# The second feed-forward product by Strassen's algorithm, in four quarters

## The chip, the core and the metric

The kernel runs on one core of one Trainium2 chip. The core has five engines that work side by side, each with a queue of its own that it takes in order: TensorE (PE) for matrix products, VectorE (DVE), ScalarE (ACT) and GpSimd (POOL) for passes over tiles, and SyncE (SP), which issues transfers. PE reads its operands from SBUF, the on-chip memory of 128 partitions, and writes to PSUM, eight banks of 128 x 512 floats; ACT and DVE bring results from there. The metric is the device time of one execution in microseconds (us). Times of single instructions come from one profiled execution.

## The reference

One layer of a streaming encoder runs over 512 tokens of width 1024. Three branches (banded attention, a gated recurrence, latent attention) are gated, summed and added to the residual. Then comes the feed-forward part, in which the change lies, and a last norm:

```python
h2 = rmsnorm(x, norm_ffn_g)
x = x + jnp.square(jax.nn.relu(h2 @ w_ff1)) @ w_ff2     # w_ff1: 1024 x 4096, w_ff2: 4096 x 1024
return rmsnorm(x, final_norm_g)
```

## The kernel before

All products have float32 accuracy made of three matmuls: each operand is split into a high part of the short float format fp32r and a low part (the rest), and high times high, high times low and low times high are added in PSUM (`mm3`, lines 223 to 226). `gemm` (line 228) does that over the 128-row blocks of the inner dimension. Activations lie transposed, features on partitions and the 512 tokens along the free dimension, so a weight block of 128 x 128 is PE's stationary operand and 512 tokens stream past it.

`stream` (line 213) brings a weight tile of 128 x 1024: SP loads it into `wr` (two buffers), ACT casts it into `wh`, DVE subtracts into `wl` (three buffers each). In the first part of the kernel, the projections, weights come in another way (`convert`, line 271): POOL issues a load of the weight, ACT negates its high part, and a second POOL transfer adds the weight to it in flight.

The feed-forward part begins at line 1154. The loop of line 1163 makes the residual `x2` (eight tiles of 128 features by 512 tokens) with `w_out`, and its scaled high and low parts `x2g`. The norm's factor per token goes through the squared ReLU, so it is applied only at the end, as `rs2`, its square. Then two halves of 2048 hidden features (line 1186): 16 products of `w_ff1` (24 matmuls of 512 columns each), relu on ACT, square on DVE and a split into `rh` and `rl`; then, for each of eight output tiles, products with `w_ff2`. The first half's 16 blocks and the third group of eight are kept as sums in `y0`. The last group's weights are split ahead (`wres`, line 1213), and its products run over 256 tokens at a time (line 1245), so that the first 256 tokens can be finished while the others are still on PE. To finish (line 1253 on) is: multiply by `rs2`, add to the residual, square for the last norm's sum, scale by the final gain on POOL; `finish_half` (line 1230) sums the squares over partitions by fp32 matmuls with a matrix of ones, makes the reciprocal root on ACT and DVE, multiplies the eight tiles (six on DVE, two on POOL) and stores them in four transfers.

PE's order is that of the code. The other queues are ordered when the program is built, by a planner that runs through the program with estimated durations and takes, for each engine, the first in priority among the instructions that are ready. Priority is the order of the code; what stands under `urgent()` (the weights) counts as 6000 places earlier.

Of the kernel before, what the change touches and what calls it, by code (L numbers as in the profile page):

```python
# [9 lines left out]
F32 = mybir.dt.float32  # L10
# [6 lines left out]
D = 1024  # L17
S = 512
# [24 lines left out]
def _blocks(w, nk, cols):  # L43

    c = w.shape[1] // cols
    return w.reshape(nk, P, c, cols).transpose(2, 1, 0, 3).reshape(c, P, nk * cols)
# [30 lines left out]
def layout(inp):  # L77
# [34 lines left out]
    o['w_out'] = _blocks(f('w_out')[0], NK, P)  # L112
    o['w_ff1'] = _blocks(f('w_ff1')[0], NK, P)
    w2 = f('w_ff2')[0]
    o['w_ff2'] = np.stack([_blocks(w2[c * 1024:(c + 1) * 1024], NK, P) for c in range(4)])
    freq = (np.float32(10000.0) ** (-np.arange(0, 32, 2, dtype=np.float32) / np.float32(32))).astype(np.float32)
    sg = np.where(np.arange(P) % 32 < 16, -1.0, 1.0).astype(np.float32)
    o['cst'] = np.concatenate([
# [20 lines left out]
def _body(ctx, tc, ap, dbgo):  # L139
# [22 lines left out]
    def acc(n="acc"):  # L162
        return ps.tile([P, S], F32, tag="acc", name=n, bufs=3)
# [990 lines left out]
    with ExitStack() as f_ctx:  # L1154
        fp = f_ctx.enter_context(tc.tile_pool(name="ffn", bufs=2, reuse_waits="tile"))

        def fw(n):
            return fp.tile([P, S], F32, tag="fw", name=n, bufs=3)


        x2, x2g = [], []
        ss = fp.tile([P, S], F32, name="fss", bufs=1)
        for m in range(NK):
            x = fqt("xres")
            nc.sync.dma_start(x, ap['xT'][m * P:(m + 1) * P, :])
            w = stream(ap['w_out'][m], eng=V)
            pz = acc("po")
            gemm(pz, w, mT, NK)
            V.tensor_tensor(x, pz, x, ALU.add)
            dbg('x2', x, m)  # L1170
            xh = fp.tile([P, S], F32R, tag="xg", name="x2h", bufs=16)
            xl = fp.tile([P, S], F32R, tag="xg", name="x2l", bufs=16)
            A.activation(xh, x, AF.Copy, scale=g_ffn[:, m:m + 1])
            V.scalar_tensor_tensor(xl, x, g_ffn[:, m:m + 1], f(xh), ALU.mult, ALU.subtract)
            x2g.append((xh, xl))
            sq = ss if m == 0 else fw("sq")
            A.activation(sq, x, AF.Square)
            if m:
                G.tensor_tensor(ss, ss, sq, ALU.add)
            x2.append(x)  # L1180
        t6 = tables("natural_log_exp_and_others", last_copy)
        rs2 = fp.tile([P, S], F32, name="rs2", bufs=1)


        y0 = []
        for half in range(2):
            rT = []
            for j in range(16):
                w = stream(ap['w_ff1'][half * 16 + j], eng=V)
                pz = acc("p1")  # L1190
                gemm(pz, w, x2g, NK)
                t = fw("t")
                A.activation(t, pz, AF.Relu)
                V.tensor_tensor(t, t, t, ALU.mult)
                rh = fp.tile([P, S], F32R, tag="r", name="rh", bufs=32)
                rl = fp.tile([P, S], F32R, tag="r", name="rl", bufs=32)
                split(rh, rl, t)
                rT.append((rh, rl))
                if half == 0 and j == 1:
                    pst = psc("pst")  # L1200
                    T.matmul(pst, ones, ss, start=True, stop=True)
                    A.activation(rs2, rstd_of(fw, pst, D, behind=t6), AF.Square)
            for m in range(NK):
                pz = acc("p2")
                gemm(pz, stream(ap['w_ff2'][2 * half, m], eng=V), rT, NK, stop=half == 1)
                if half == 0:
                    gemm(pz, stream(ap['w_ff2'][1, m], eng=V), rT[8:], NK, start=False)
                    t = act.tile([P, S], F32, tag="act", name="y0")
                    A.copy(t, pz)
                    y0.append(t)  # L1210
                else:
                    V.tensor_tensor(y0[m], y0[m], pz, ALU.add)
        wres = []
        for m in range(NK):
            if m >= 6:
                hi, lo = stream(ap['w_ff2'][3, m], eng=V)
                wres.append([(hi[:, i * S:(i + 1) * S], lo[:, i * S:(i + 1) * S]) for i in range(2)])
                continue
            r = ws.tile([P, 1024], F32, tag="wr", name="wr", bufs=2)
            nc.sync.dma_start(r, ap['w_ff2'][3, m])  # L1220
            hl = []
            for i in range(2):
                if m < 2:
                    hi, lo = (act.tile([P, S], F32R, tag="act", name=n) for n in ("wrh", "wrl"))
                else:
                    hi, lo = (fp.tile([P, S], F32R, tag="xg", name=n, bufs=16) for n in ("wrh", "wrl"))
                split(hi, lo, r[:, i * S:(i + 1) * S])
                hl.append((hi, lo))
            wres.append(hl)
        def finish_half(n):  # L1230
            pst = psc("pst")[:, :256]
            T.matmul(pst, ones, ss[:, n], start=True, stop=False)
            T.matmul(pst, ones, sql, start=False, stop=True)
            rf = rstd_of(fw, pst, D, w=256)
            for i in range(NK // 2):
                o = fp.tile([P, 2, 256], F32, tag="r", name="o", bufs=32)
                for j in range(2):
                    m = 2 * i + j
                    (G if m in (2, 5) else V).tensor_tensor(o[:, j], x2[m][:, n], rf, ALU.mult)
                nc.sync.dma_start(ap['out'][2 * i * P:2 * (i + 1) * P, n].rearrange("(a p) c -> p a c", p=P), o)  # L1240

        for m in range(NK):
            V.tensor_tensor(y0[m], y0[m], rs2, ALU.mult)
            V.tensor_tensor(x2[m], x2[m], y0[m], ALU.add)
        for sh in range(2):
            n = slice(sh * 256, sh * 256 + 256)
            for m in range(NK):
                pz = acc("p3")[:, :256]
                for i in range(2):
                    gemm(pz, wres[m][i], rT[8 + 4 * i:], 4, n0=sh * 256, n=256, start=i == 0, stop=i == 1)  # L1250
                if sh and m == 1:
                    finish_half(slice(0, 256))
                V.tensor_tensor(y0[m][:, n], pz, rs2[:, n], ALU.mult)
                V.tensor_tensor(x2[m][:, n], x2[m][:, n], y0[m][:, n], ALU.add)
                sq = ss[:, n] if m == 0 else fw("sq")[:, :256]
                A.activation(sq, x2[m][:, n], AF.Square)  # L1256
                if m == NK - 1:
                    sql = sq
                elif m:
                    V.tensor_tensor(ss[:, n], ss[:, n], sq, ALU.add)  # L1260
                G.tensor_tensor(x2[m][:, n], x2[m][:, n], g_fin[:, m:m + 1].to_broadcast([P, 256]), ALU.mult)  # L1261
        finish_half(slice(256, 512))

# [14 lines left out]
```

## Time and profile before

| | us |
|---|---|
| three timed runs: median (lowest to highest) | 959.55 (958.98 to 963.6) |
| the profiled execution, its own time | 955.7 |
| its span, first to last instruction | 953.9 |
| PE busy | 915.7 |
| DVE busy | 595.6 |
| ACT busy | 494.5 |
| POOL busy | 183.5 |
| mean granted TensorE clock | 0.995 of full speed |

Busy times of different engines overlap, so they are not to be added. A matmul's row is longer than the distance to the next one, as matmuls are pipelined; the distance is what a stream of them costs. The first product begins at 589.01, the last matmul of the second product ends its slot at 941.47.

### The profile page before, as it was taken

Reading aid. Unit: us, or ns where it says so; the run is one execution under the profiler, and the core shown is the slowest. Engines: PE = TensorE matmul, PEld = TensorE weight load, DVE = VectorE, ACT = ScalarE, POOL = GpSimd, SP = SyncE. Lnnn points to the kernel's source line nnn. Section 1 sums busy time; section 2 is a strip of 40 time slices with the busy share of each in tenths; the row PEclk is TensorE's granted clock in tenths of the full one; section 3 lists DMA queues with packets and bytes.
Section 4 is the critical chain, followed back from the end, with each engine's and each line's share of the span. In section 5 each row is a group of like instructions: output and inputs, shape, how many; then the busy total and the mean of one; then the engine's idle time right before and its main releaser. Section 6 shows DMA issues by size and latency. Waiting matters only on the chain.

```text
span 953.9 us, 12608 instructions
## 1 busy us (share of the span) xinstructions
PE 915.7 (96%) x4682; PEld 773.2 (81%) x4682; DVE 595.6 (62%) x1134; ACT 494.5 (52%) x911; POOL 183.5 (19%) x248
## 2 busy tenths in 40 slices
PE   8799999998998999999999999999999999999995
PEld 6578898887877787878788888888888888888994
DVE  6688888787788869788452644544322234446755
ACT  7567778887675767667542434434322233342311
POOL 4422111111163434342122022000000000000032
PEclk9999999999999999999999999999999999999998
DMA  6966445565666564858699532232232322322402
GB/s 201 220 138 125 88 94 112 122 144 116 139 130 135 120 147 91 191 114 179 139 239 194 136 111 89 88 111 89 93 106 88 104 95 89 111 89 91 153 1 89
DMA packets 37181, 117.04 MB, mean 123 GB/s; under 512 B 4416, under 2 KB 8656, under 8 KB 37120
## 3 DMA queue, kind: packets, MB, share of 16 engines
q0 software_dynamic: 18496, 67.17, 33.2%
q1 hardware_dynamic: 18624, 49.06, 15.7%
q8 instruction: 37, 0.61, 0.2%
q14 instruction: 24, 0.20, 0.1%
HBM read 114.05 MB, written 2.16 MB: 122 GB/s over the span
## 4 chain that ended last, share of the span: by engine, by line
PE 71%; DVE 15%; issue 4%; ACT 4%; DMA 3%; POOL 2%; SPq 0%; DVEq 0%; POOLq 0%; ACTq 0%
PE p L226 12%; PE p L225 12%; PE p L224 12%; PE pj L323 3%; PE pj L319 3%; PE pj L321 3%; PE pg L321 2%; PE pg L319 2%; PE pg L323 2%; PE sc L520 2%; DVE qbl L211 2%; PE po L226 2%; PE po L224 2%; PE po L225 2%; DMA bias<-in_rel 2%
## 5 line engine op out<-in xcount | busy, mean ns | idle before, releaser
L220 DVE TENSOR_TENSOR wl<-wr,wh 128x1024 fp32r<-128x1024 f32 x66 | 80.8, 1224 | 145.0 <-ACT wh L219 140.8
L219 ACT CAST wh<-wr 128x1024 fp32r<-128x1024 f32 x66 | 69.5, 1053 | 174.0 <-PE p L225 136.5
L224 PE MATMUL p<-x2h,wh 128*128 128x512 f32 x256 | 100.0, 391 | 0.0
L226 PE MATMUL p<-x2h,wl 128*128 128x512 f32 x256 | 99.6, 389 | 0.0
L225 PE MATMUL p<-x2l,wh 128*128 128x512 f32 x256 | 99.6, 389 | 0.0
L277 ACT ACTIVATE wl<-wh 128x1024 fp32r<-128x1024 f32 x64 | 67.7, 1058 | 47.6 <-PE pg L323 26.4
L224 PE MATMUL p<-rh,wh 128*128 128x512 f32 (+1 forms) x224 | 83.7, 374 | 0.0
L225 PE MATMUL p<-rl,wh 128*128 128x512 f32 (+1 forms) x224 | 83.7, 374 | 0.0
L226 PE MATMUL p<-rh,wl 128*128 128x512 f32 (+1 forms) x224 | 83.7, 374 | 0.0
L1261 POOL TENSOR_TENSOR xres<-xres,cst 128x256 f32<-128x256 f32 x16 | 13.1, 822 | 335.7 <-ACT fss L1256 309.5
L319 PE MATMUL pg<-xgh,wh 128*128 128x512 f32 x192 | 75.7, 394 | 0.3 <-DVE tg L882 0.3
L321 PE MATMUL pg<-xgl,wh 128*128 128x512 f32 x192 | 75.8, 395 | 0.0
L323 PE MATMUL pg<-xgh,wl 128*128 128x512 f32 x192 | 75.6, 394 | 0.0
L319 PE MATMUL pj<-xgh,wh 128*128 128x512 f32 x160 | 64.6, 404 | 2.0 <-ACT c L427 2.0
L321 PE MATMUL pj<-xgl,wh 128*128 128x512 f32 x160 | 65.2, 407 | 0.0
L323 PE MATMUL pj<-xgh,wl 128*128 128x512 f32 x160 | 63.8, 398 | 1.1 <-DMA wl<-in_w_aqk 1.1
L225 PEld LDWEIGHTS p<-x2l,wh 128*128 128x128 f32 x256 | 48.1, 188 | 10.3 <-issue 0.2
L224 PEld LDWEIGHTS p<-x2h,wh 128*128 128x128 f32 x256 | 48.1, 188 | 10.2 <-issue 0.2
L226 PEld LDWEIGHTS p<-x2h,wl 128*128 128x128 f32 x256 | 48.1, 188 | 9.9
L224 PEld LDWEIGHTS p<-rh,wh 128*128 128x128 f32 x224 | 42.2, 188 | 7.5
L225 PEld LDWEIGHTS p<-rl,wh 128*128 128x128 f32 x224 | 42.2, 188 | 7.5
L226 PEld LDWEIGHTS p<-rh,wl 128*128 128x128 f32 x224 | 42.2, 188 | 7.4
(380 smaller groups left out, 2397.4 us busy)
## 6 DMA issues: line engine op xcount, KB each, us to landing
wr<-in_w_ff SPq DMA_DIRECT2D x64, 512.0 KB, 3.3
wh<-in_w_g POOLq DMA_DIRECT2D x24, 512.0 KB, 4.0
wl<-in_w_g POOLq DMA_DIRECT2D x24, 512.0 KB, 6.1
wh<-in_w_br POOLq DMA_DIRECT2D x12, 512.0 KB, 3.6
wl<-in_w_br POOLq DMA_DIRECT2D x12, 512.0 KB, 5.8
wh<-in_w_aqk POOLq DMA_DIRECT2D x8, 512.0 KB, 4.6
wl<-in_w_aqk POOLq DMA_DIRECT2D x8, 512.0 KB, 6.5
wr<-in_w_out SPq DMA_DIRECT2D x8, 512.0 KB, 3.3
```

What stands on the lines that cost most here:

```text
L211: V.tensor_tensor(lo, src, f(hi), ALU.subtract)
L219: A.copy(hi[:, :n], r[:, :n])
L220: (eng or G).tensor_tensor(lo[:, :n], r[:, :n], f(hi[:, :n]), ALU.subtract)
L224: T.matmul(out, wh, xh, start=start, stop=False, **kw)
L225: T.matmul(out, wh, xl, start=False, stop=False, **kw)
L226: T.matmul(out, wl, xh, start=False, stop=stop, **kw)
L277: A.activation(lo, f(hi), AF.Copy, scale=-1.0)
L319: T.matmul(out, wh, xh, start=start, stop=False, **kw)
L321: T.matmul(out, wh, xl, start=False, stop=False, **kw)
L323: T.matmul(out, wl, xh, start=False, stop=stop, **kw)
L520: T.matmul(sc[:, :n], l[:, t * P:(t + 1) * P], r[:, :n], start=i == 0, stop=i == len(scores) - 1)
L1261: G.tensor_tensor(x2[m][:, n], x2[m][:, n], g_fin[:, m:m + 1].to_broadcast([P, 256]), ALU.mult)
```

## The change

Strassen's algorithm (in Winograd's form) multiplies matrices of 2 x 2 blocks with seven block products in place of eight. The second product is cut into four quarters of 1024 hidden features. In a quarter the tokens are halved (256), the hidden features are halved (two times 512), and the outputs are halved (two times 512). `first(q)` makes the hidden features in pairs of blocks, one from each half, and from their four quarters of 128 x 256 the three plain operands (A11, A12, A22) and four sums (S3, S1, S2, S4), all split into high and low. The weights' sums are made by `chain`: SP loads one block into a float tile, POOL transfers add others, and between uses `parts` splits what the tile holds. `product` does one of the seven, 4 x 4 tiles of 256 columns, three matmuls each. Products that share a term are added in the same PSUM banks (`start` False); `take` copies or adds the banks to the four quarters of the output, which are kept over the quarters of hidden features. The outputs of the first three are added to the residual within the last `first` (`residual`), those of the last after its products (`resid`, `squares`). The scaling by the final gain goes from POOL to ACT, the hidden features' squares from DVE to ACT. The last norm's squares go into three sums in place of two, and the last product of all runs tile by tile (`tiles_first`).

In the diff, lines with "..." mark what is left out; the old second product stands in the code above.

```diff
@@ -112,7 +112,9 @@
     o['w_out'] = _blocks(f('w_out')[0], NK, P)
     o['w_ff1'] = _blocks(f('w_ff1')[0], NK, P)
     w2 = f('w_ff2')[0]
-    o['w_ff2'] = np.stack([_blocks(w2[c * 1024:(c + 1) * 1024], NK, P) for c in range(4)])
+    w2 = w2.reshape(4, 2, 2, 2, P, 2, S).transpose(0, 3, 5, 1, 4, 2, 6)
+    o['w_ff2'] = w2.reshape(4, 2, 2, 2, P, 2 * S)
     freq = (np.float32(10000.0) ** (-np.arange(0, 32, 2, dtype=np.float32) / np.float32(32))).astype(np.float32)
     sg = np.where(np.arange(P) % 32 < 16, -1.0, 1.0).astype(np.float32)
     o['cst'] = np.concatenate([
@@ -1154,12 +1156,15 @@
...
+        temps = [yt("t0"), yt("t1"), fp.tile([P, S], F32, name="t2", bufs=1)]
         def fw(n):
-            return fp.tile([P, S], F32, tag="fw", name=n, bufs=3)
+            temps.append(temps.pop(0))
+            return temps[-1]
...
-        ss = fp.tile([P, S], F32, name="fss", bufs=1)
+        ss = yt("fss")
...
-        y0 = []
-        for half in range(2):
-            rT = []
...
+        A11, A12, A22, S3, S1, S2, S4 = range(7)
+        H = 256
+        rs2 = yt("rs2")
+        def pair(x):
+            return x.rearrange("p (a c) -> p a c", a=2)
+        def first(q):
+            ops = []
+            for i in range(4):
+                rh = fp.tile([P, 7, H], F32R, tag="rh", name="rh", bufs=4)
+                rl = fp.tile([P, 7, H], F32R, tag="rl", name="rl", bufs=4)
+                r = fp.tile([P, 8, H], F32, tag="rf", name="rf", bufs=1)
+                a21 = r[:, 7]
+                for j in range(2):
+                    w = stream(ap['w_ff1'][q * 8 + 2 * i + j], eng=V)
+                    pz = acc("p1")
+                    gemm(pz, w, x2g, NK)
+                    t = r[:, 0:8:7] if j == 0 else r[:, A12:A22 + 1]
+                    A.activation(t, pair(pz), AF.Relu)
+                    A.activation(t, t, AF.Square)
+                    if q == 0 and i == 0 and j == 1:
+                        pst = psc("pst")
+                        T.matmul(pst, ones, ss, start=True, stop=True)
+                        A.activation(rs2, rstd_of(fw, pst, D, behind=t6), AF.Square)
+                A.copy(rh[:, 0:3], r[:, 0:3])
+                V.tensor_tensor(r[:, S3:S1 + 1], r[:, 0:3:2], a21.unsqueeze(1).to_broadcast([P, 2, H]), ALU.subtract)
+                V.scalar_tensor_tensor(r[:, S2], r[:, S1], -1.0, r[:, A11], ALU.mult, ALU.subtract)
+                V.scalar_tensor_tensor(r[:, S4], r[:, S2], -1.0, r[:, A12], ALU.mult, ALU.subtract)
+                V.tensor_tensor(rl[:, 0:3], r[:, 0:3], f(rh[:, 0:3]), ALU.subtract)
+                A.copy(rh[:, 3:7], r[:, 3:7])
+                V.tensor_tensor(rl[:, 3:7], r[:, 3:7], f(rh[:, 3:7]), ALU.subtract)
+                ops.append((rh, rl))
+                if q == 3:
+                    residual(i)
+            return ops
+        def parts(r):
+            hi = ws.tile([P, 1024], F32R, tag="wh", name="wh")
+            lo = ws.tile([P, 1024], F32R, tag="wl", name="wl")
+            A.copy(hi, r)
+            V.tensor_tensor(lo, r, f(hi), ALU.subtract)
+            return hi, lo
+        def chain(src, steps, tag, n):
+            with urgent():
+                ts = [fp.tile([P, 1024], F32, tag=tag, name=tag, bufs=2) for _ in range(2)]
+                for b in range(2):
+                    nc.sync.dma_start(ts[b], src[b])
+                    for a in steps[:n]:
+                        G.dma_start(ts[b], a[b], accum_op=ALU.add)
+            rest = list(steps[n:])
+            def step():
+                with urgent():
+                    w = []
+                    a = rest.pop(0) if rest else None
+                    for b in range(2):
+                        w.append(parts(ts[b]))
+                        if a is not None:
+                            G.dma_start(ts[b], a[b], accum_op=ALU.add)
+                return w
+            return step
+        def product(banks, w, ops, x, start, tiles_first=False):
+            order = [(i, t) for i in range(4) for t in range(4)]
+            if tiles_first:
+                order = [(i, t) for t in range(4) for i in range(4)]
+            for i, t in order:
+                wh, wl = w[i // 2]
+                c = slice(i % 2 * S + t * P, i % 2 * S + t * P + P)
+                rh, rl = ops[i]
+                mm3(pair(banks[t // 2])[:, t % 2], wh[:, c], wl[:, c], rh[:, x], rl[:, x],
+                    start and i == 0 and t % 2 == 0, i == 3, skip_group_check=True)
+        where = dict(c11=(0, 0, ALU.add), m12=(0, 1, ALU.subtract), c21=(1, 0, ALU.add), m22=(1, 1, ALU.subtract))
+        out = {}
+        def take(name, banks):
+            if name in out:
+                for b in range(2):
+                    V.tensor_tensor(out[name][b], out[name][b], banks[b], ALU.add)
+            else:
+                out[name] = [act.tile([P, S], F32, tag="act", name=name) for _ in range(2)]
+                for b in range(2):
+                    A.copy(out[name][b], banks[b])
+        def resid(name, b, src, ts=(0, 1)):
+            th, ch, op = where[name]
+            n = slice(th * H, th * H + H)
+            u = out[name][b]
+            k = slice(ts[0], ts[-1] + 1)
+            V.tensor_tensor(pair(u)[:, k], pair(src)[:, k], rs2[:, n].unsqueeze(1).to_broadcast([P, len(ts), H]), ALU.mult)
+            for t in ts:
+                m = ch * 4 + 2 * b + t
+                V.tensor_tensor(x2[m][:, n], x2[m][:, n], pair(u)[:, t], op)
+        def residual(i):
+            name = ('c11', 'm12', 'c21', 'm22')[i]
+            for b in range(2):
+                resid(name, b, out[name][b])
+        sqs = {}
+        def squares(name, b, ts=(0, 1)):
+            th, ch, _ = where[name]
+            n = slice(th * H, th * H + H)
+            for t in ts:
+                m = ch * 4 + 2 * b + t
+                sq = sqs.setdefault(th, [])
+                if len(sq) < 2:
+                    d = fin[th][:, len(sq)]
                 else:
...
+                    d = fw("sq")[:, :H]
+                A.activation(d, x2[m][:, n], AF.Square)
+                sq.append(d)
+                if 2 < len(sq) < NK:
+                    V.tensor_tensor(sq[len(sq) % 2], sq[len(sq) % 2], d, ALU.add)
+                A.activation(x2[m][:, n], x2[m][:, n], AF.Copy, scale=g_fin[:, m:m + 1])
+        def finish_half(th):
+            n = slice(th * H, th * H + H)
+            pst = ptp("pst")[:, :H]
+            sq = sqs[th]
+            for i, d in enumerate((sq[0], sq[1], sq[-1])):
+                T.matmul(pst, ones, d, start=i == 0, stop=i == 2)
+            rf = rstd_of(fw, pst, D, w=H)
             for i in range(NK // 2):
...
+                o = fp.tile([P, 2, H], F32, tag="xg", name="o", bufs=16)
                 for j in range(2):
                     m = 2 * i + j
                     (G if m in (2, 5) else V).tensor_tensor(o[:, j], x2[m][:, n], rf, ALU.mult)
                 nc.sync.dma_start(ap['out'][2 * i * P:2 * (i + 1) * P, n].rearrange("(a p) c -> p a c", p=P), o)
...
+        for q in range(4):
+            last = q == 3
+            (b11, b12), (b21, b22) = ([ap['w_ff2'][q, i, j] for j in range(2)] for i in range(2))
+            ts = chain(b11, [b12, b22, b21], "cw", 1)
+            t3 = chain(b22, [b12], "ew", 1)
+            ops = first(q)
+            if last:
+                out.clear()
+                fin = [pair(fp.tile([P, S], F32, tag="xg", name="fin", bufs=16)) for _ in range(2)]
+                left = [fp.tile([P, S], F32, tag="xg", name="left", bufs=16) for _ in range(2)]
+            def plain(b):
+                return [stream(b[i], eng=V) for i in range(2)]
+            ba = [psc("sa") for _ in range(2)]
+            bc = [ptp("sc") for _ in range(2)]
+            product(ba, plain(b11), ops, A11, True)
+            take('c11', ba)
+            product(bc, ts(), ops, S1, True)
+            take('m22', bc)
+            bb = [pup("sb"), acc("sb")]
+            product(bb, plain(b21), ops, A12, True)
+            take('c11', bb)
+            if last:
+                for b in range(2):
+                    resid('c11', b, out['c11'][b])
+                    squares('c11', b)
+            product(ba, ts(), ops, S2, False)
+            take('m12', ba)
+            product(bc, plain(b22), ops, S4, False)
+            take('m12', bc)
+            if last:
+                for b in range(2):
+                    resid('m12', b, out['m12'][b])
+                    squares('m12', b)
+            product(ba, t3(), ops, S3, False)
+            take('m22', ba)
+            if last:
+                finish_half(0)
+                for b in range(2):
+                    resid('m22', b, out['m22'][b])
+                    squares('m22', b)
+                out['c21'] = left
+                for b in range(2):
+                    resid('c21', b, ba[b])
+            else:
+                take('c21', ba)
+            bb = [pup("sb"), acc("sb")]
+            product(bb, ts(), ops, A22, True, tiles_first=last)
+            if last:
+                for b in range(2):
+                    for t in range(2):
+                        resid('c21', b, bb[b], (t,))
+                        squares('c21', b, (t,))
+            else:
+                take('c21', bb)
+        finish_half(1)
```

## Rows read from the trace of the kernel before

**Rows 1.** The page, busy time of each engine, its share, its instructions.

```profile
PE 915.7 (96%) x4682; PEld 773.2 (81%) x4682; DVE 595.6 (62%) x1134; ACT 494.5 (52%) x911; POOL 183.5 (19%) x248
```

**Rows 2.** The page, the chain that ended last, by engine.

```profile
PE 71%; DVE 15%; issue 4%; ACT 4%; DMA 3%; POOL 2%; SPq 0%; DVEq 0%; POOLq 0%; ACTq 0%
```

**Rows 3.** Stretches: window, length, each engine's busy time (instructions), clock, DMA share, GB/s.

```profile
589.01:676.05 87.04, 87.04 (x384) 71.73 (x383) 42.35 (x51) 37.23 (x52) 1.78 (x1) 1.00 0.28 95
895.00:941.00 46.00, 46.00 (x383) 45.90 (x382) 27.69 (x58) 10.78 (x22) 14.17 (x17) 1.00 0.15 50
```

**Rows 4.** Timeline of PE, start and duration in us: the 256-column stretch.

```profile
894.55 0.28 PE L224 MATMUL p<-rh,wrh 128*128 128x256 f32 x1
894.66 0.28 PE L225 MATMUL p<-rl,wrh 128*128 128x256 f32 x1
894.78 0.28 PE L226 MATMUL p<-rh,wrl 128*128 128x256 f32 x1
...
941.47 0.59 PE L1232 MATMUL pst<-fss,ones 128*128 128x256 f32 x2
```

**Rows 5.** Groups by line from 545 on: busy us, mean ns; idle before, releaser.

```profile
L220 DVE TENSOR_TENSOR wl<-wr,wh 128x1024 fp32r<-128x1024 f32 x64 | 78.4, 1224 | 140.8 <-ACT wh L219 140.8
L219 ACT CAST wh<-wr 128x1024 fp32r<-128x1024 f32 x64 | 67.4, 1053 | 171.2 <-PE p L225 136.5 <-issue 31.7 <-PE p L226 2.1
L211 DVE TENSOR_TENSOR rl<-t,rh 128x512 fp32r<-128x512 f32 x32 | 22.2, 693 | 21.4 <-ACT rh L210 21.3
L210 ACT CAST rh<-t 128x512 fp32r<-128x512 f32 x32 | 19.9, 621 | 44.2 <-DVE t L1194 44.2
L1212 DVE TENSOR_TENSOR y<-y,p 128x512 f32<-128x512 f32 x8 | 5.5, 687 | 12.7 <-PE p L226 12.7
L1260 DVE TENSOR_TENSOR fss<-fss,sq 128x256 f32<-128x256 f32 x12 | 5.1, 425 | 5.4 <-ACT sq L1256 5.4
```

**Rows 6.** Timeline of ACT after a block of the first product.

```profile
769.40 1.05 ACT L219 CAST wh<-wr 128x1024 fp32r<-128x1024 f32 x1 [3.91 <-PE p L225]
770.35 0.59 ACT L1193 ACTIVATE t<-p 128x512 f32<-128x512 f32 x1
```

**Rows 7.** Timeline of DVE, passes one after the other.

```profile
927.52 3.60 DVE L1239 TENSOR_TENSOR o<-xres,st_r 128x256 f32<-128x256 f32 x6
...
931.49 0.42 DVE L1254 TENSOR_TENSOR xres<-xres,y 128x256 f32<-128x256 f32 x1
931.84 0.41 DVE L1253 TENSOR_TENSOR y<-p,rs 128x256 f32<-128x256 f32 x1
```

**Rows 8.** Timeline of all engines behind the last matmul.

```profile
942.13 0.42 DVE L1254 TENSOR_TENSOR xres<-xres,y 128x256 f32<-128x256 f32 x1
942.65 0.42 ACT L1256 ACTIVATE sq<-xres 128x256 f32<-128x256 f32 x1 [2.46 <-DVE xres L1254]
943.12 0.70 PE L1233 MATMUL pst<-sq,ones 128*128 128x256 f32 x2 [1.05 <-ACT sq L1256]
...
946.71 3.15 DVE L1239 TENSOR_TENSOR o<-xres,st_r 128x256 f32<-128x256 f32 x6
```

**Rows 9.** DMA queues, and transfers: KB each, median us from issue to landing.

```profile
q1 hardware_dynamic: 18624, 49.06, 15.7%
...
wr<-in_w_ff SPq DMA_DIRECT2D x64, 512.0 KB, 3.3
...
wl<-in_w_g POOLq DMA_DIRECT2D x24, 512.0 KB, 6.1
```

**Rows 10.** Timeline of SP's queue from 380 to 546.

```profile
399.90 85.90 SPq L1165 DMA_DIRECT2D xres<-in_xT  x8
529.18 13.55 SPq L216 DMA_DIRECT2D wr<-in_w_out  x4
```

**Rows 11.** Stretches behind PE's last matmul, columns as in rows 3.

```profile
945.00:950.00 5.00, 0.00 (x0) 0.00 (x0) 4.00 (x8) 0.66 (x2) 1.68 (x2) 0.73 0.19 62
950.00:954.00 4.00, 0.00 (x0) 0.00 (x0) 0.00 (x0) 0.00 (x0) 0.00 (x0) 0.50 0.55 184
```

More of the change, by code (lines that the diff above doesn't have):

```diff
@@ L1181, in _body @@
         t6 = tables("natural_log_exp_and_others", last_copy)
-        rs2 = fp.tile([P, S], F32, name="rs2", bufs=1)
-        y0 = []
-        for half in range(2):
-            rT = []
[L1188 to L1210, printed above, removed]
-                else:
-                    V.tensor_tensor(y0[m], y0[m], pz, ALU.add)
@@ L1213, in _body @@
[L1213 to L1234, printed above, removed]
+        A11, A12, A22, S3, S1, S2, S4 = range(7)
[32 more added lines that the diff above has]
+            return ops
@@ L1235, in finish_half @@
+        def finish_half(th):
[5 more added lines that the diff above has]
+            rf = rstd_of(fw, pst, D, w=H)
             for i in range(NK // 2):
-                o = fp.tile([P, 2, 256], F32, tag="r", name="o", bufs=32)
+                o = fp.tile([P, 2, H], F32, tag="xg", name="o", bufs=16)
                 for j in range(2):
@@ L1240, in finish_half @@
                 nc.sync.dma_start(ap['out'][2 * i * P:2 * (i + 1) * P, n].rearrange("(a p) c -> p a c", p=P), o)
[L1242 to L1261, printed above, removed]
@@ L1262, in _body @@
-        finish_half(slice(256, 512))
+        for q in range(4):
[52 more added lines that the diff above has]
+                take('c21', bb)
```

## The prediction

> **What bounds the kernel now.** I read the page's busy times first: PE is busy 915.7 of 953.9 us, DVE 595.6, ACT 494.5 [rows 1]. A share that high says that the sum of the matmuls sets the time, so the chain of waits came next: it runs through PE for 71% and through DVE for 15% [rows 2], the rest being ends and turns. Then the stages. [...] In the stretch with 256 columns it is 46.00 of 46.00 us with 383: 0.120 us each [rows 3]. Two starts one after the other lie 0.11 to 0.12 apart, and the 384 of that part fill 894.55 to 941.47, 46.92 us; what is over 384 x 0.120 is 0.84, the two fp32 column sums for the first half's norm, 0.42 each [rows 4]. [...] DVE has slack in that stretch (27.7 of 46 us), ACT more (10.8). Last the end: from the last matmul's slot at 941.47 to 953.9, 12.4 us, a string of dependent steps with no engine full [rows 4, 8].
>
> The profiled execution took 955.7 us, span 953.9; the sum is made against it. The three timed runs have a median of 959.55, 3.9 above; I carry the difference over to that median.
>
> **What goes and comes on PE.** Now the second product is 576 matmuls of 512 columns and 384 of 256: 576 x 0.2267 + 384 x 0.120 = 130.6 + 46.1 = 176.7 us. Afterwards it is 4 quarters x 7 products x 16 tiles x 3 = 1344 matmuls of 256: 161.3 us. The columns fall by an eighth, the time by 8.7%, since all now pay the dearer short form. **Gain 15.4.** The first product keeps its 768 matmuls. Each half's norm sum takes three fp32 matmuls in place of two: 0.42 each, +0.4 for the half that stands inside PE's order (the other half's is in the end below).
>
> **Weights.** A product eats two 1024-column tiles, one per 24 x 0.120 = 2.88 us. Three hi/lo buffers let tile n be split from 2.88 x (n-2), so its cast (1.05) and subtraction (1.22) [rows 5] have 5.76 us and need 2.3: hidden, slack 3.4. Per product ACT has 2.1 of 5.76 us of that, DVE 2.4, and at most four more passes of 0.69 for the sums. The adding transfers are POOL's; the nearest row, an adding load of the projections, lands in 6.1 us, a plain one in 3.3 [rows 9]. Between the uses of one sum buffer there are two products, 11.5 us, at the least; a split, then 6.1, leaves 3 us. Taken at nothing; without the cover each late tile would stop PE by its lateness, from 0 to 6 us. [...]
>
> **Making the operands.** For each pair of blocks: relu and square on ACT, sums S1 to S4 on DVE, two casts, two subtractions. A pair has 10.88 us of PE time; ACT needs about 6.4 with the two weight casts, DVE 6.2 (in the last quarter 9.1 with the residual passes). The single raw buffer makes the next pair's relu wait about 1.5 us, which the three PSUM banks hide. Only the last pair of a quarter is short: product 1 wants its first operand after 36 matmuls, 4.3 us. A weight cast goes ahead of the relu: the row shows the cast at 769.40 and the relu at 770.35 [rows 6]. From the block's end: cast 0.95, relu 0.6, square 0.6, then the subtraction for S3 and S1 (0.69), S2 (0.43) and the low part of 768 columns (between 0.69 and 1.22 [rows 5], about 0.95), with two crossings: 4.3 to 4.9. Bounds 0 and 0.6 a quarter, or 1.5 if a second weight subtraction comes between. **I take 1.0 for four.**
>
> **The end.** This term decides. In the last quarter the residual, the squares' sums and the output all fall on DVE within the last three products. An independent DVE pass over 256 columns comes 0.35 after the one before (931.49, 931.84), one over 512 about 0.62; six output passes took 3.60 beside POOL's two [rows 7]. After product 5's last matmul DVE owes:
> - two weight subtractions, 2.3; four PSUM sums (the second takes of m12 and m22), 2.4
> - the residual passes of m12, m22 and of c21's first part: six pairs of tiles at 0.62 + 2 x 0.35, 7.9
> - c21's second part, four at 0.70, 2.8; eight sums of squares, 2.8
> - first half's norm, three passes, 1.2, and six output passes, 3.3
>
> Together 22.7; the last residual stands near 22.4 in the order that the code asks for, as nearly every pass has its input long before. PE, in the same time, has products 6 and 7 (11.5), three sums (1.3) and one wait: the sums stand in PE's order between products 6 and 7, and need m12's squares, whose chain on DVE (take, multiply, add, two weight subtractions between, square on ACT, add) ends about 7.9 after product 5, when product 6 took 5.76. **PE waits 2.1** (bounds 0.5 and 3); product 7 is queued behind it. So PE is through at 14.9, DVE 7.5 later. From the last residual on everything is as before: 942.55 (942.13 + 0.42) to 953.9 [rows 8], 11.35, plus 0.4 for the third sum. The end after the last matmul thus grows from 12.4 to 7.5 + 11.35 + 0.4 = 19.2. **Loss 6.8**; bounds +1 (DVE keeps up; two tiles instead of one after the last matmul) and +9 (POOL's passes hold DVE up more).
>
> PE would be idle some 7 us before the last sums. [...]
>
> The scaling by the final gain moves from POOL to ACT: 16 passes of 0.42 us, behind which ACT, with 13 us of work in the last 22, delays nothing.
>
> **Sum:** -15.4 + 0.4 + 1.0 + 2.1 + 6.8 = -5.1 us. 955.7 becomes 950.6; the median, 954.5.
>
> **Rivals.**
> A. *The end stays on PE.* If DVE's passes fit beside products 6 and 7, loss and wait go but for 1: -15.4 + 0.4 + 1 + 1 = -13, 946.5. For it: DVE is half idle now. Against: the list above, of which 14 us can't begin before product 6 ends, while product 7 lasts 5.8.
> B. *Waits in every quarter.* Operands or sums 1.5 to 3 us late at one turn of each quarter, by the in-order queues of ACT and DVE: +6 to +12 less the 1.0 taken, -0.1 to +6: 959.5 to 965.5. For it: no slack at product 1. Against: the 3 us everywhere else.
> C. *Slower: the next quarter's first w_ff1 tile stands behind the sums' loads in SP's queue.* In program order four loads for the sum buffers precede it. The second waits for the last read of the old sum: product 7's second tile, whose buffer comes free halfway through product 6 at 31.7 after product 1's start, split at 34.0. Behind it come two more and then the tile: 512 KB take 1.6 us at the queue's own rate (49.06 MB in 15.7% of the span) [rows 9], so it lands at 34.0 + 3 x 1.6 + 3.3 = 42.1, cast 43.2, when PE wants it at 40.3: 2.9 lost, to 6 where adding transfers run between. Three turns: 9 to 18, so +4 to +13, 963 to 972. It decides once the tile's issue comes later than 36 after product 1's start. Against: SP's queue goes by what is ready. The residual's loads (line 1165) were issued from 399.9 to 485.5, all before the first w_out tile at 529.18, though that one is marked urgent and seven of the eight follow it in the code [rows 10]. The tile's own buffer is free some 14 us before the second sum load's, so it should go first.
>
> **From this to the numbers.** Forecast 0.57, A 0.13, B 0.17, C 0.13. The forecast's own bounds (0 to 2 at product 1, +4 to +9 at the end, 0.5 to 3 for the wait) give 950 to 958.5. 0.5%, 4.8 us, is about what a measurement here can tell from no change. The forecast lies just beyond it, so half of its chance counts as faster: with A, 0.43. Same: the other half, most of B, a little of C, 0.41. Slower: 0.16. The range 946.5 to 963 reaches to A and through most of B.
>
> **What would show it.** Right: product stretches with 48 matmuls in 5.8 us and no gaps; a gap of about 2 us on PE before product 7; DVE without idle time from product 5 to the last residual, 7 us after the last matmul; w_ff1's first tile of a quarter issued before the sums' second load. Wrong: PE waiting on a weight cast at a quarter's start (C) or at each product 1 by over 1.5 us (B); the last residual within 2 us of the last matmul (A).

## The result, and the profile after

The changed kernel takes 952.99 us (median of seven runs, 951.21 to 957.54); the kernel before, run beside it, 959.55 (seven runs, 957.63 to 963.62). The ratio is 0.9926, with a 95% interval of 0.9904 to 0.9948: 7.1 us less, between 5.0 and 9.2. The prediction was 954.5, faster by 5.1. The profiled execution took 951.3, with a span of 949.5.

The page's busy times answer to [rows 1], its chain of waits by engine to [rows 2]:

```profile
PE 907.1 (96%) x5070; PEld 784.4 (83%) x5070; DVE 657.1 (69%) x1212; ACT 557.5 (59%) x983; POOL 201.4 (21%) x264
```

```profile
PE 72%; DVE 15%; issue 4%; DMA 4%; ACT 3%; POOL 1%; SPq 0%; DVEq 0%; POOLq 0%; ACTq 0%
```

PE's share is still 96%, and DVE is busy 61.5 us more. Next come stretches of the changed kernel's span (columns as in [rows 3]: window, length, busy time of PE, weight load, DVE, ACT and POOL with their instructions, granted clock, DMA share, GB/s), and from the view of waits the only line that PE has behind the start of the first product:

```profile
589.00:760.00 171.00, 171.00 (x1069) 154.99 (x1068) 98.69 (x113) 86.65 (x106) 16.18 (x17) 1.00 0.57 150
760.00:870.00 110.00, 110.00 (x648) 98.08 (x647) 72.60 (x97) 52.00 (x62) 7.72 (x9) 1.00 0.61 166
...
917.00:925.00 8.00, 7.61 (x58) 7.02 (x57) 7.94 (x15) 5.00 (x10) 0.00 (x0) 1.00 0.01 2
925.00:930.50 5.50, 5.42 (x46) 5.21 (x44) 5.50 (x16) 3.68 (x10) 2.65 (x1) 1.00 0.15 51
930.50:936.50 6.00, 0.00 (x0) 0.00 (x0) 6.00 (x18) 2.64 (x7) 2.38 (x2) 0.76 0.39 131
936.50:939.70 3.20, 2.90 (x6) 1.85 (x6) 0.79 (x4) 1.57 (x4) 0.00 (x0) 0.50 0.00 0
```

```profile
PE pst L1325 <- DVE fin L1317: 6.7, 2, 6.3
```

PE runs through the quarters without a gap. It waits twice, both times for the sum of squares: 0.4 us before the first half's norm and 6.3 before the second half's. In the 6 us of 930.5 to 936.5 PE does nothing and DVE is busy for all of it: the end belongs to DVE. The granted clock was 0.76 over that stretch and 0.50 in the next, 936.5 to 939.7.

**Where the time went.** The work ahead of the first product is the same in both kernels, yet that product starts at 589.01 in the profiled execution of before and at 591.86 in that of after. One difference is in the view of stretches: from 20 to 40 us the clock was 0.83 after and 1.00 before. It is not the whole of it: in experiments 1 and 4 below it was 0.91 there, and the product starts at 593.20 and 594.70. What else moves the start stays open. The profiled execution of before was an unusually smooth one: its mean clock was 0.995, while 18 further runs of the same kernel beside two of the experiments had 0.982 to 0.991, and the seven runs of after 0.981 to 0.989. So I compare from the first product's start to the end of the span. That stage took 953.9 - 589.01 = 364.9 us before and 949.5 - 591.86 = 357.6 after: -7.3, beside the -7.1 of the ratio.

### The profile page after: what moved, and what is told of

It is laid out like the page before. It is cut to its first block, busy times and chain, and to the rows that moved or that the text cites. A ratio compares the mean times of both kernels' runs of the same rounds, so it can differ in the third digit from the quotient of the medians.

```text
span 949.5 us, 13636 instructions
## 1 busy us (share of the span) xinstructions
PE 907.1 (96%) x5070; PEld 784.4 (83%) x5070; DVE 657.1 (69%) x1212; ACT 557.5 (59%) x983; POOL 201.4 (21%) x264
## 4 chain that ended last, share of the span: by engine, by line
PE 72%; DVE 15%; issue 4%; DMA 4%; ACT 3%; POOL 1%; SPq 0%; DVEq 0%; POOLq 0%; ACTq 0%
PE p L227 6%; PE p L228 6%; PE p L226 6%; PE pj L325 3%; PE pj L321 3%; PE pj L323 3%; PE pg L321 3%; PE pg L325 3%; PE pg L323 3%; PE sa L228 2%; PE sa L227 2%; PE sa L226 2%; PE sc L522 2%; DMA bias<-in_rel 2%; PE po L227 2%
## 5 line engine op out<-in xcount | busy, mean ns | idle before, releaser
L221 ACT CAST wh<-wr 128x1024 fp32r<-128x1024 f32 x64 | 67.2, 1050 | 111.0 <-PE p L227 24.8
L222 DVE TENSOR_TENSOR wl<-wr,wh 128x1024 fp32r<-128x1024 f32 x64 | 78.3, 1223 | 75.9 <-ACT wh L221 67.5
L1256 POOL DMA_DIRECT2D cw<-in_w_ff x16 | 13.7, 858 | 219.2 <-DVE wl L1236 216.4
L227 PE MATMUL sa<-rl,wh 128*128 128x256 f32 x192 | 54.3, 283 | 0.0
L228 PE MATMUL sa<-rh,wl 128*128 128x256 f32 x192 | 54.3, 283 | 0.0
L226 PE MATMUL sa<-rh,wh 128*128 128x256 f32 x192 | 54.3, 283 | 0.0
L1236 DVE TENSOR_TENSOR wl<-cw,wh 128x1024 fp32r<-128x1024 f32 x24 | 29.3, 1223 | 29.9 <-ACT wh L1235 29.9
L1235 ACT CAST wh<-cw 128x1024 fp32r<-128x1024 f32 x24 | 25.2, 1050 | 35.0 <-PE sc L227 11.1
L321 PEld LDWEIGHTS pg<-xgh,wh 128*128 128x128 f32 x192 | 36.9, 192 | 7.8 <-DVE tg L884 0.4
```

The source lines that it names most:

```text
L221: A.copy(hi[:, :n], r[:, :n])
L222: (eng or G).tensor_tensor(lo[:, :n], r[:, :n], f(hi[:, :n]), ALU.subtract)
L226: T.matmul(out, wh, xh, start=start, stop=False, **kw)
L227: T.matmul(out, wh, xl, start=False, stop=False, **kw)
L228: T.matmul(out, wl, xh, start=False, stop=stop, **kw)
L321: T.matmul(out, wh, xh, start=start, stop=False, **kw)
```

## The experiments

All start from the changed kernel. Each result is given as that stage, whose 357.6 is the mark, since starts differ between executions (591.9 to 596.1 in the experiments). Experiments 1 to 5 are one execution each. How well the stage repeats is seen in the part that no edit touches: from the first product's start to the end of product 7's last slot it takes 338.40 us in the changed kernel and in experiments 1 to 4 and 6 alike.

**1. c21 summed in PSUM.** In the last quarter product 7 goes on adding in the banks that hold c21's first part, so DVE has no passes on that part.

```diff
-                for b in range(2):
-                    resid('c21', b, ba[b])
...
-            bb = [pup("sb"), acc("sb")]
-            product(bb, ts(), ops, A22, True, tiles_first=last)
+            bb = ba if last else [pup("sb"), acc("sb")]
+            product(bb, ts(), ops, A22, not last, tiles_first=last)
```

> In the last quarter product 7 goes on adding in the banks of product 6, so c21 needs one residual pass in place of two: DVE is spared two passes of 512 columns and four of 256 behind product 6, 2 x 0.60 + 4 x 0.34 = 2.6 us. Theory 1 (DVE's list of passes sets the end): from the first product's start to the end, 357.5 us with the change, comes to 355.0 +- 0.6, and the last residual stands 2.6 us closer to the last matmul. Theory 2 (a chain of dependent steps sets the end, and DVE only looks full): 357.5 +- 0.5. PE's order and its wait before product 7 stay as they are in both.

Measured: 593.20 to 949.1, 355.9: -1.7, between the ranges of the two theories (355.6 at most, 357.0 at least). The last residual came 1.9 earlier, though the passes taken away amount to 2.6. The timeline of this kernel's ACT, POOL and DVE (in brackets the idle time before, and who ended it):

```profile
929.20 5.09 POOL L1331 TENSOR_TENSOR o<-xres,t 128x256 f32<-128x256 f32 x2 [22.07 <-DVE t L251]
...
934.33 0.72 ACT L1314 ACTIVATE t<-xres 128x256 f32<-128x256 f32 x2 [1.63 <-POOL o L1331]
934.77 0.76 DVE L1317 TENSOR_TENSOR fin<-fin,t 128x256 f32<-128x256 f32 x2 [0.73 <-ACT t L1314]
...
936.24 0.43 DVE L1294 TENSOR_TENSOR xres<-xres,left 128x256 f32<-128x256 f32 x1
```

POOL's two output passes held the first half's norm factor, in one of the rotating temporaries `t`, for 5.09 us; ACT's next square needed that tile, and DVE stood 0.73 us for that square, which is what the 1.9 lacks of 2.6. DVE's passes do set the end, but with fewer of them a temporary is late next.

**2. First half's outputs last.** The eight output passes and four stores of the first half come after the last residual (the factor is kept in a tile of its own), so DVE has 2.0 us less before it.

```diff
-                finish_half(0)
+                rf0 = norm_half(0)
...
-        finish_half(1)
+        outputs(0, rf0)
+        outputs(1, norm_half(1))
```

> The first half's output passes (six on DVE, two on POOL) are put behind the last residual in the code; the factor they need is kept in tiles of its own. Theory 1: the last residual comes 2.0 us earlier (six passes of 0.34), the passes fall into DVE's 2.4 us wait for the last sums, and the end comes 1.5 to 2.0 us earlier: 355.5 to 356.0 from the first product's start. Theory 2: no gain, 357.5, or up to 1 us lost where the passes stand before the second half's norm.

Measured: 591.87 to 948.1, 356.2: -1.4, 0.2 short of the first theory's range, with the last residual 1.5 earlier. POOL's two passes were not put off, since POOL had nothing else to do. DVE and POOL here, from the timeline, the like passes of the changed kernel in the second fence:

```profile
927.87 2.03 POOL L1336 TENSOR_TENSOR o<-xres,st_r 128x256 f32<-128x256 f32 x2 [22.07 <-DVE st_r L251]
928.28 0.68 DVE L1291 TENSOR_TENSOR left<-sa,rs 128x512 f32<-128x512 f32 x1
928.88 1.30 DVE L1317 TENSOR_TENSOR fin<-fin,t 128x256 f32<-128x256 f32 x2
```

```profile
927.85 5.03 POOL L1331 TENSOR_TENSOR o<-xres,t 128x256 f32<-128x256 f32 x2 [22.06 <-DVE t L251]
927.93 2.10 DVE L1331 TENSOR_TENSOR o<-xres,t 128x256 f32<-128x256 f32 x6
```

In the changed kernel DVE's six passes kept their pace (2.10 us) and POOL's two took 5.03; at the very end of the span it is the other way round, with 3.16 for DVE's six and 1.73 for POOL's two. In experiment 2 POOL took 2.03 and DVE's two additions 1.30 instead of 0.75. In each of the three places the passes of one of the two engines took longer; of the 2.0 us taken off DVE's list 0.55 went there, and 1.45 was left as gain.

**3. PE kept at work.** 48 matmuls whose result nobody reads follow product 7.

```diff
+        wt = acc("keep")
+        for _ in range(48):
+            T.matmul(wt[:, :H], ops[0][0][:, A11, :P], ops[0][0][:, A11], start=True, stop=True)
         finish_half(1)
```

> 48 matmuls of 256 columns into a bank that nobody reads follow the last product, so that PE runs on for 5.8 us while DVE works off its list. Theory 1 and the clock: the last residual stays where it is, the last three sums run at the upper level and take 1.7 us instead of 2.9, and the end comes 1.2 us earlier, 356.3 from the first product's start. If the lower clock costs nothing there: 357.5.

Measured: 593.37 to 949.9, 356.5: -1.1. PE's timeline in the changed kernel and, below, in the experiment:

```profile
936.71 2.04 PE L1325 MATMUL pst<-fin,ones 128*128 128x256 f32 x4 [6.30 <-DVE fin L1317]
938.55 1.06 PE L1325 MATMUL pst<-t,ones 128*128 128x256 f32 x2
```

```profile
931.77 5.92 PE L1392 MATMUL keep<-rh 128*128 128x256 f32 x48
938.24 1.10 PE L1325 MATMUL pst<-fin,ones 128*128 128x256 f32 x4 [0.55 <-DVE fin L1317]
939.27 0.70 PE L1325 MATMUL pst<-t,ones 128*128 128x256 f32 x2
```

The sums took 1.73 us from first start to last end instead of 2.90. So the fallen clock (0.50 in 936.5 to 939.7 of the changed kernel, against 1.00 here in 935 to 940) cost 1.2 us.

**4. No adding transfers.** The sum tiles hold their first block alone.

```diff
-                    for a in steps[:n]:
-                        G.dma_start(ts[b], a[b], accum_op=ALU.add)
...
-                        if a is not None:
-                            G.dma_start(ts[b], a[b], accum_op=ALU.add)
```

> The adding transfers are left out (the weights' sums then hold their first block alone, which is another result). If they are hidden, as the prediction costed them: 357.5 +- 0.3 from the first product's start, and PE without a gap in the quarters in both. If their load on the DMA engines or POOL's queue held weights back anywhere, it comes out shorter, by up to 6 us.

Measured: 594.70 to 952.4, 357.7: no difference. The adding transfers cost nothing here, as the prediction had it.

**5. w_ff1's tiles behind the sums' loads.** The order of rival C is forced: in quarters 2 to 4 the first two tiles of w_ff1 are issued after the second load of `cw`.

```diff
-            nc.sync.dma_start(r[:, :n], src)
+            ld = nc.sync.dma_start(r[:, :n], src)
+            if held:
+                after(ld, held.pop())
...
+            if q:
+                held.append(loads_of[-2])
+                held.append(loads_of[-2])
```

> SP's queue is made to issue the first two w_ff1 tiles of quarters 2 to 4 behind the second load of the new sum buffer, the order that rival C supposed. By C's own price PE stops 2.9 to 6 us at each of the three turns: 9 to 18 us, 366.5 to 375.5 from the first product's start in place of 357.5. By the trace of the changed kernel less, as there the other two sum loads go 5 us before: the tile would be issued at 34 us after product 1's start, land 3.5 to 7 later and be cast by 38.6 to 42, when PE wants it at 40.3: 0 to 2 us a turn, 357.5 to 363.5. If the weights have slack everywhere: 357.5.

Measured: 594.64 to 976.0, 381.4: +23.7, more than either theory allowed. PE's waits behind the first product in this kernel, its timeline at the first turn, and stretches there:

```profile
PE p L230 <- ACT wh L225: 14.3, 3, 6.5
PE p L232 <- DVE wl L226: 0.5, 1, 0.5
```

```profile
673.15 0.33 SPq L1250 DMA_DIRECT2D cw<-in_w_ff  x1
673.53 20.19 SPq L220 DMA_DIRECT2D wr<-in_w_ff  x5
...
684.98 2.12 ACT L225 CAST wh<-wr 128x1024 fp32r<-128x1024 f32 x2 [9.85 <-DMA wr<-in_w_ff]
686.08 0.79 PE L230 MATMUL p<-x2h,wh 128*128 128x512 f32 x1 [6.54 <-ACT wh L225]
```

```profile
679.30:686.10 6.80, 0.26 (x3) 0.06 (x2) 0.36 (x2) 1.09 (x2) 0.86 (x1) 0.72 1.06 297
686.10:690.00 3.90, 3.86 (x8) 2.62 (x9) 2.92 (x3) 1.00 (x1) 0.00 (x0) 0.50 0.82 196
690.00:694.00 4.00, 4.00 (x14) 3.13 (x13) 1.23 (x1) 1.05 (x1) 0.00 (x0) 0.68 0.59 155
```

The wait is the one that rival C described, a weight cast at a quarter's start, three times: from the end of product 7's last slot to the first matmul of w_ff1 it is 6.7, 3.6 and 4.5 us, 14.8 together (14.3 in the view, which counts from the end of a row): within its 9 to 18. Its price was too low in two places. The tile, issued at 673.53, was there at 684.98, 11.4 us later where 3.3 was counted: the DMA share was 0.87 from 670 to 679.3 and 1.06 from there to 686.1, with the sums' loads and adding transfers under way. And behind each gap the clock was lower for a while (0.50 from 686.1 to 690 and 0.68 to 694; 0.74 in 776 to 780 and 0.58 in 866 to 870, around the ends of the other two): w_ff1's 192 matmuls of these three quarters take 46.9, 46.0 and 46.6 us, where the changed kernel's take 43.55. That is 8.8 together, 0.5 of it the second wait above, and 14.8 + 8.8 = 23.6.

**6. Experiments 1 and 2 together**, as a version to keep.

> e1 and e2 in one. Theory 1: 2.6 + 2.0 us less of DVE's passes before the last residual, so it comes some 2 us behind the last matmul, PE then pauses too shortly for its clock to fall and the last sums take 1.7 in place of 2.9: 5.8 us less, 351.7 from the first product's start; the ratio to the kernel before about 0.9865 in place of 0.9926. Theory 2: the ratio stays at 0.9926 +- 0.0022.

Measured: 596.05 to 948.9, 352.85: -4.8, where the two alone gave -1.7 and -1.4. Time: 949.31 us (six runs, 945.68 to 953.9) beside 961.41 of the kernel before (eleven runs, 959.14 to 965.4); ratio 0.9876, 0.9845 to 0.9907, which holds the 0.9865 of the first theory and not the 0.9926 of the second, though it just touches the range around that. The stage itself misses the first theory's 351.7 by 1.1. DVE and PE at the end, from the timeline, and one stretch:

```profile
937.01 0.41 DVE L1294 TENSOR_TENSOR xres<-xres,left 128x256 f32<-128x256 f32 x1
937.14 0.70 PE L1327 MATMUL pst<-fin,ones 128*128 128x256 f32 x2 [0.58 <-DVE fin L1317]
```

```profile
932.00:939.00 7.00, 4.68 (x28) 3.30 (x27) 6.90 (x21) 5.47 (x14) 3.08 (x2) 1.00 0.04 14
```

The last residual ends 3.0 us after product 7's last slot, which ends at 934.45, where it was 7.0 in the changed kernel. The clock was 1.00 from 932 to 939, PE being busy for 4.68 of these 7.00 us, and the row of the last sum (two matmuls) is 0.70 us long, where with either edit alone the clock was 0.50 in 935 to 940 and the row is 1.06. Of the 4.8 us, 4.0 are gained before the last residual (1.9 and 1.5 by the two alone) and 0.8 behind it, where neither alone gained any: most of the more-than-additive gain lies where the clock stayed up. The factor's own tile of experiment 2 is also what experiment 1 was short of.

**7. The last quarter plain.** Three quarters by Strassen; the last 1024 hidden features are multiplied plainly, with resident split weights and the finishing of the kernel before.

```diff
-        for q in range(4):
-            last = q == 3
+        for q in range(3):
+            last = False
...
+                for i in range(2):
+                    gemm(pz, wres[m][i], rT[4 * i:], 4, n0=sh * H, n=H, start=i == 0, stop=i == 1)
```

> Three quarters by Strassen as in the changed kernel; the last quarter's 1024 hidden features are multiplied plainly, in 256-column form with weights split ahead, and finished as the kernel before does it (gain on POOL, sums of squares in one tile), so that no Strassen sums stand in the end. Theory 1 (the end of the changed kernel is long because the last quarter's residual, sums and outputs fall on DVE within three products): PE pays 5.8 us more in the last quarter (384 matmuls of 256 columns, 46.1, for 40.3), the wait before product 7 goes and the end after the last matmul falls from 19.1 back to 12.4. First product to the end: 174.1 + 0.9 + 3 x 40.3 + 46.1 + 0.8 + 12.4 = 355.3 us, where the changed kernel has 357.6; up to 1 us more if the first operand of the plain part is late. Theory 2 (the long end has another cause, such as the clock or the transfers): the end stays near 19 and the stage costs 5.8 us more, 362 to 363.

Measured: 593.13 to 948.2, 355.1, as the first theory said (355.3). Time: 953.43 us (four runs) beside 963.79 (seven); ratio 0.9891, 0.9847 to 0.9934. The only wait of PE behind the first product, and the end in the timeline:

```profile
PE pst L1429 <- ACT t L1460: 1.1, 1, 1.1
```

```profile
936.06 0.59 PE L1428 MATMUL pst<-fss,ones 128*128 128x256 f32 x2
937.70 0.70 PE L1429 MATMUL pst<-t,ones 128*128 128x256 f32 x2 [1.05 <-ACT t L1460]
```

From the last product's end, 936.06, to the end of the span are 12.1 us, the 12.4 of the kernel before. So the long end belongs to Strassen's passes in the last quarter and the finishing that goes with them (the edit took back both), and there they cost more than they save: the plain quarter costs PE 5.8 us more, and all of that and 2.5 more comes back. With the finishing of experiment 6 it is Strassen's last quarter that leads again, 352.85 to 355.1, by the stage of one execution each; the intervals of the two ratios overlap, so that the times do not show it.

## Why the prediction was right, point by point

**The sum.** In the stage its terms now read: first product 768 x 0.2267 = 174.1, the norm within it 0.9, Strassen's products 161.3, the turn before product 7 2.1, the end 19.2: 357.6, and 357.6 was measured (the experiments' expectations have 19.1 and 357.5, from the end of the last row instead of its slot). The stage lost 7.3 where the sum had lost 5.1. The forecast's median was 1.5 too high. The 2.2 between the stages are the two terms below that were taken too high. One bound has a slip: the forecast's own lowest terms add up to 949.0 us, not 950.

**The products: right.** With no gap on PE from the first product to product 6, and product 6's and the first product's starts where 0.120 and 0.2267 a matmul put them, the gain of 15.4 is there whole. The 0.2267 and the 0.120 are PE's busy times in [rows 3] over their 384 matmuls of 512 columns and 383 of 256; in the changed kernel 192 matmuls of w_ff1 take 43.55 us, 0.2268 each, and product 6's 48 take 5.76, 0.120 each. No rival's wait appears in the quarters.

**Product 1's operands: mis-sized.** "Bounds 0 and 0.6 a quarter, or 1.5 if a second weight subtraction comes between. I take 1.0 for four." It was 0. DVE's timeline in the changed kernel's first quarter, and, from PE's, the matmul that wants the last pair's low part:

```profile
639.56 0.95 DVE L1224 TENSOR_TENSOR rl<-rf,rh 128x768 fp32r<-128x768 f32 x1
640.43 1.22 DVE L1236 TENSOR_TENSOR wl<-cw,wh 128x1024 fp32r<-128x1024 f32 x1
...
640.71 0.28 PE L227 MATMUL sa<-rl,wh 128*128 128x256 f32 x1
```

Product 1's first matmul starts at 636.28, and the low part is wanted 37 matmuls later, at 640.71; it is ready at 640.51. From the weight cast's start at 636.25 the chain takes 4.26 us, the lower end of the 4.3 to 4.9 worked out. The second weight subtraction does come, but behind the low part. The slack of 0.2 us is thin.

**The turn before product 7: mis-sized.** "PE waits 2.1 (bounds 0.5 and 3)", and three sums of 0.42 beside it, 3.4 together. PE's timeline there:

```profile
922.29 0.28 PE L228 MATMUL sa<-rh,wl 128*128 128x256 f32 x1
922.96 1.28 PE L1325 MATMUL pst<-fin,ones 128*128 128x256 f32 x4 [0.39 <-DVE fin L1317]
924.08 0.59 PE L1325 MATMUL pst<-t,ones 128*128 128x256 f32 x2
...
924.63 0.28 PE L227 MATMUL sb<-rl,wh 128*128 128x256 f32 x1
```

Product 6's last slot ends at 922.41 and product 7's stream begins about 924.5: 2.1 in all, so beside 1.3 for the sums the wait was 0.8. Most of the 1.3 that was counted too much is DVE's chain: its last addition (at 923.07 in DVE's timeline below) ends at 923.49, 6.8 us after product 5's last slot (916.65), where 7.9 was worked out. The rest is an overlap: the first of the three sums begins at 922.96, while DVE still adds; the prediction let all three wait for the last.

**The end: right, by errors that cancel.** Predicted 19.2, measured 949.5 - 930.26 = 19.2. The mechanism holds: DVE has next to no idle time from product 5's end to the last residual (7.94 of 8.00 us, 5.50 of 5.50 and 6.00 of 6.00 in the stretches above):

```profile
916.13 1.41 DVE L1279 TENSOR_TENSOR m<-m,sc 128x512 f32<-128x512 f32 x2
...
923.07 0.42 DVE L1317 TENSOR_TENSOR fin<-fin,t 128x256 f32<-128x256 f32 x1
923.40 1.28 DVE L1279 TENSOR_TENSOR m<-m,sa 128x512 f32<-128x512 f32 x2
...
933.15 1.08 DVE L1294 TENSOR_TENSOR xres<-xres,left 128x256 f32<-128x256 f32 x3
...
936.82 0.41 DVE L1294 TENSOR_TENSOR xres<-xres,left 128x256 f32<-128x256 f32 x1
```

But the list of DVE's passes was 1.8 us too long. The last residual ends at 937.23, 20.6 after product 5's last slot, where 22.4 was counted. 1.3 of that are the first half's six output passes: 3.3 was counted, after the 3.60 beside POOL's two in [rows 7], and they took 2.0 (927.93 to 929.94), while POOL's two took 5.03. 0.5 is the first pass, which begins at 916.13, before product 5 is through. PE was through 1.3 earlier as well, so the last residual comes 7.0 after product 7 (7.5 predicted), and from there to the end it is 12.3 us (11.35 [rows 8] + 0.4 predicted): two errors of 0.5 that cancel. That the end came out to 0.1 us is luck. The second error is the clock, for which the sum has no term, though it had fallen behind PE's last matmul in the kernel before too [rows 11]: here it was 0.50 after 6 us without work for PE, and experiment 3 put the price at 1.2 us. Without that the stretch is shorter than predicted: 11.1 us in experiment 3, as the first of the three sums starts before the last residual is done.

**The rivals.** A fell by the trace: the last residual came 7.0 us after the last matmul, not within 2. B fell by PE's waits. C's order did not occur, for the reason given: the tile with the free buffer goes first. SP's queue in the changed kernel at the first turn:

```profile
655.97 3.21 SPq L218 DMA_DIRECT2D wr<-in_w_ff  x2
661.72 3.21 SPq L1244 DMA_DIRECT2D ew<-in_w_ff  x2
667.49 3.20 SPq L1244 DMA_DIRECT2D cw<-in_w_ff  x2
673.25 0.33 SPq L218 DMA_DIRECT2D wr<-in_w_ff  x1
```

The two tiles issued from 655.97 on are w_ff1's first two of the second quarter; the sums' loads come behind them. Experiment 5 shows that C was a real risk and that 963 to 972 was too cheap for it: 23.7 us on the changed kernel's median is 976.7.

**The adding transfers.** The prediction took them at nothing, with 6.1 us for one to land. DMA issues of the changed kernel, from the first product on (KB each, median us from issue to landing):

```profile
wr<-in_w_ff SPq DMA_DIRECT2D x52, 512.0 KB, 3.5
cw<-in_w_ff POOLq DMA_DIRECT2D x22, 512.0 KB, 5.6
ew<-in_w_ff SPq DMA_DIRECT2D x6, 512.0 KB, 3.6
ew<-in_w_ff POOLq DMA_DIRECT2D x6, 512.0 KB, 8.5
cw<-in_w_ff SPq DMA_DIRECT2D x6, 512.0 KB, 7.9
```

Those into `cw` land in 5.6, under the 6.1 assumed; those into `ew` take 8.5, but the plain loads issued next to them take 7.9 too. At the first turn both fall where the DMA engines are busy (share 0.80 in 667.5 to 673.2, 1.07 in 673.2 to 680); that may be why, but it was not shown. Experiment 4 shows that none of it reaches PE.

**What stays open.** Whether experiment 6 beats the changed kernel by its stage's 4.8 us in the median was not measured side by side; the two ratios differ by 0.5%, and their intervals touch. Its gain is split above by where it falls, not by cause: no run gives the factor its own tile and changes nothing else.

## What to carry to other kernels

Where a method saves matmuls by adding passes on other engines, cost it once for the middle, where the passes have cover, and once for the last round, where everything those engines owe comes after the last matmul: here the first three quarters kept their whole gain, and the last one, as it was first written, lost more than its own. List the passes that the busiest engine of the end owes, in order, against PE's time; such a list named the right engine here, though it was 1.8 of 22.4 us too long and only other errors made the total fit. Then look at what holds that list's temporaries, and at the first load of the next round in its queue.

## What the runs showed of the hardware

- Where POOL's two output passes ran beside DVE's passes, those of one of the two engines took longer. In the changed kernel POOL's two took 5.03 us while DVE ran six multiplications and some additions; at the end of the span POOL's two took 1.73 and DVE's six 3.16 instead of 2.10; in experiment 2 POOL's took 2.03 and DVE's next two additions 1.30 instead of 0.75. What decides which engine it is was not shown: in all three places POOL's first pass begins (927.85, 942.51, 927.87) during a DVE pass, and only in the first did POOL's take long.
- In experiment 5 a gap on PE cost more than its length. After a wait of 6.5 us the clock was 0.50 for the next 3.9 us and 0.68 for 4 more, and the 192 matmuls behind the gap took 46.9 us instead of 43.55: 3.3 us on top.
- A 512 KB load, which in the changed kernel lands in 3.5 us as a median, took 11.4 in experiment 5, where it was issued behind four other loads and beside adding transfers, with the DMA share at 0.87 and then 1.06.
- The clock dipped within a stretch that is the same in both programs (0.83 in 20 to 40 us of the changed kernel's execution, 0.91 in experiments 1 and 4, 1.00 in the kernel before), and the start of the part under study lay anywhere from 589.0 to 596.1. A difference between two profiles is best read from the stage that was changed.
